# Attention probabilities copied block by block by DMA into F32R slots before they are turned; the merged sum of the branches kept in DRAM

## The chip, the cores and the metric

The kernel runs on one core of a Trainium2 chip. A core has a matrix engine (PE, which loads a 128x128 block of stationary weights and streams moving columns through it; the loads are listed as PEld), a vector engine (DVE), a scalar engine (ACT), a general engine (POOL), and a queue engine (SP) that issues most of the DMAs. PE writes into eight PSUM banks; everything else lives in SBUF (128 partitions) or in DRAM. Engines run side by side, each in the order of its own instructions, and wait for each other by semaphores.

The metric is the device time of one execution in microseconds (us), the median of the runs. Times quoted from the trace come from one profiled execution.

## The reference, cut to what matters

One decoder layer on 512 positions, width 1024. Three mixers read the same normalised input, their outputs are gated and summed, and a feed-forward part follows. The change touches the attention mixer (branch B) and the gated sum:

```python
h = rms_norm(x, g_pre_mix)
z = h @ w_in                      # u, v, q, kv, nsa_g, xr, rg, mg
y_a = gmlp_mixer(...)             # chunked spatial gating
y_b = nsa_mixer(...)              # attention: 16 heads, 4 key/value groups
y_c = rglru_mixer(...)            # linear recurrence

# inside nsa_mixer, for each group of 4 heads and both of "selected" and "window":
s = jnp.where(mask, einsum(q, k) * scale, NEG_INF)
o = einsum(softmax(s), v)
y_b = g0 * o_cmp + g1 * o_slc + g2 * o_win

gates = sigmoid(mg)
merged = gates[0] * (y_a @ w_br_a) + gates[1] * (y_b @ w_br_b) + gates[2] * (y_c @ w_br_c)
x = x + rms_norm(merged @ w_o, g_post_mix)
x = x + rms_norm(swiglu(rms_norm(x)))
```

With 512 positions, 8 selection blocks and a top 16, every block is selected, so the selected and the window attention are both plain causal attention over the same 512 keys, with different key and value projections.

## The kernel before

Everything is kept with channels on the partitions and the 512 positions along the row. Most matrix products are made from two parts of each operand: `split` (L114) has ACT write the rounded part `hi` as type F32R and DVE the remainder `lo`, and three products (hi by hi, hi by lo, lo by hi) replace one exact product. [...]

The program has three phases with their own SBUF and PSUM pools (`PHASES`, `BANKS`). Phase 1 is attention, with two banks `sc` for scores, three `tr` for transposes, one `o` for outputs and two `mm` for other products. Big buffers that live across phases have tags of their own; tag `m` has two buffers of four rows each, and before the change they hold `merged`, the gated sum of the branches, from branch C (phase 0) through attention to branch B (phase 2).

Attention runs over four groups of heads. For each group there are six units of work (class `Unit`, L884): query tile 0 and 1 with both branches at once, tile 2 and 3 with one branch each. A unit has three steps:

- `scores(j)` (L900), for each of its four heads: PE multiplies queries and keys into a bank `sc` (L910), DVE takes the mask and the maximum (L914), ACT the exponential with its sum (L916), all into the buffer `P` (two buffers). After the fourth head DVE makes the factors (L919, L921), and ACT (L926, two heads) and DVE (L930, the others) scale the probabilities in `P`.
- `turn(br, kt)` (L932): for one block of 128 keys, four transposes on PE (L935, one for each head; a "turn" below is one such transpose) from `P` through the f32 identity `ident` into a bank `tr`, which `split` takes apart into `ph` and `pl`.
- `values(br, kt)` (L940): two products with the values `V` into the bank `o` (L948).

A group has 2 + 4 + 3 + 3 + 4 + 4 = 20 blocks, so there are 80 blocks and 320 turns in all.

`attention` (L972) interleaves these steps with the other matrix products that must be made: the projections of the next group and the gates and products of branch A (`fill`). It counts slots, one for each six products of the fill; `LAG_T` is the least number of slots between a unit's last score and its first turn, `LAG_V` that between a block's turn and its product with `V`. Behind that, the framework's scheduler lays out the final order on each engine; rows of it are shown with the change.

SP issues the weight loads (`raw`, two buffers, L182) in the order of `wload`, and the copies between partitions of the queries `q` (L789) and keys `K` (L802).

Branch A's gate is a row of tag `tg` with one buffer in phase 1: ACT writes it (`gate_part`, L1067), DVE multiplies it with the branch's product (`branch_part`, L1079; L1090) and adds it to `merged` (L1091). Behind attention, branch B does the same and splits the sum into `mh` and `ml`, which the output projection reads.

Of the kernel before, what the change touches and what calls it, by code (L numbers as in the profile page):

```python
# [22 lines left out]
F32 = mybir.dt.float32  # L23
# [6 lines left out]
S = 512  # L30
D = 1024
NK = 8
# [18 lines left out]
def hybrid_block(ctx: ExitStack, tc: tile.TileContext, A, out):  # L51
# [18 lines left out]
    def next_banks(i):  # L70
        if psum[0]:
            psum[0].__exit__(None, None, None)
        psum[0] = tc.tile_pool(name=f"psum{i}", bufs=1, space=PSUM, reuse_waits="tile")
        psum[1:] = psum[0].__enter__(), BANKS[i]
# [18 lines left out]
    def slab(name, dt=F32, tag="slab", shape=(4, S)):  # L93
        pool, bufs = (merge if tag == "m" else big, TAGS[tag]) if tag in TAGS else phase_pool[tag]
        return pool.tile([128, *shape], dt, tag=tag, name=nm(name), bufs=bufs)

    def row(name, dt=F32, tag="row"):
        pool, bufs = phase_pool[tag] if tag in phase_pool else (mid, 6)
        return pool.tile([128, S], dt, tag=tag, name=nm(name), bufs=bufs)

    def bank(tag):
        return psum[1].tile([128, S], F32, tag=tag, name=nm(tag), bufs=psum[2][tag])
# [10 lines left out]
    def f32(ap):  # L113
        return ap.bitcast(F32)  # L114

    def split(src, hi, lo, lo_eng=None):
        res["hi"] = SC.activation(hi, src, AF.Copy)  # L117
        e = lo_eng or V
        if e is GP:
            GP.tensor_sub(lo, src, f32(hi))  # L120
        else:
            res["lo"] = V.tensor_sub(lo, src, f32(hi))  # L122
# [761 lines left out]
    class Unit:  # L884

        po = {}

        def __init__(self, g, a, brs):  # L890
            self.g, self.a, self.brs, self.n = g, a, brs, 128 * (a + 1)
            self.blocks = [(br, kt) for br in brs for kt in range(a + 1)]
            self.last = (1, a)
            self.pt = {}

        def part(self, j, br):
            o = self.brs.index(br) * self.n
# [2 lines left out]
        def scores(self, j):  # L900
            g, a, n, brs = self.g, self.a, self.n, self.brs
            w = len(brs)
            if j == 0:
                self.T = slab("P", tag="P")
                self.st = mid.tile([128, 3, 4, w], F32, tag="ast", name=nm("ast"), bufs=3)
            st, K = self.st, at[g]["k"]
            ps = bank("sc")
            lhs = at[g]["q"][:, j, a * 128:(a + 1) * 128]
            for i in range(2):
                PE.matmul(ps[:, :w * n].rearrange("p (b n) -> p b n", b=w), lhs, K[:, i, brs[0]:brs[-1] + 1, :n],  # L910
                          start=(i == 0), stop=(i == 1))
            for b, br in enumerate(brs):
                t = self.part(j, br)
                V.tensor_tensor_reduce(out=t, in0=ps[:, b * n:b * n + n], in1=mask[0][:, S - n:], scale=-0.125,  # L914
                                       scalar=3.0e38, op0=OP.add, op1=OP.min, accum_out=st[:, 0, j, b:b + 1])
                SC.activation(t, t, AF.Exp, scale=-1.0, bias=st[:, 0, j, b:b + 1],  # L916
                              accum_out=st[:, 1, j, b:b + 1])
            if j == 3:
                V.reciprocal(st[:, 2], st[:, 1])  # L919
                gt = gates[:, a, 12 * g:12 * g + 12].rearrange("p (h b) -> p h b", b=3)  # L920
                V.tensor_mul(st[:, 2], st[:, 2], gt[:, :, 1 + brs[0]:2 + brs[-1]])  # L921

                own = 0 if w == 2 else 2
                for i in range(own):
                    t = self.part(i, brs[0])
                    SC.activation(t, t, AF.Copy, scale=st[:, 2, i, 0:1])  # L926
                for b, br in enumerate(brs):
                    o = b * n
                    t = self.T[:, own:4, o:o + n]
                    V.tensor_tensor(t, t, st[:, 2, own:4, b:b + 1].to_broadcast([128, 4 - own, n]), op=OP.mult)  # L930

        def turn(self, br, kt):  # L932
            pt = bank("tr")
            for j in range(4):
                PE.transpose(pt[:, j * 128:(j + 1) * 128], self.part(j, br)[:, kt * 128:(kt + 1) * 128], ident)  # L935
            ph, pl = row("ph", F32R), row("pl", F32R)
            split(pt, ph, pl)
            self.pt[br, kt] = ph, pl
# [23 lines left out]
                    ready.add(g)  # L962

    mask = [None]

    def mask_in():
        mask[0] = slab("mask", tag="mask", shape=(S,))
        GP.memset(mask[0], 0.0)
        GP.affine_select(mask[0][:, 384:], mask[0][:, 384:], pattern=[[-1, 128]], compare_op=OP.is_ge,
                         fill=-1e30, base=0, channel_multiplier=1)  # L970

    def attention(fills):  # L972


        slot = [0]
        LAG_T, LAG_V, LAG_C, LAG_K = 3, 3, 2, 3

        def steps(g, slots):

# [83 lines left out]


    mg = {}

    def gate_part(b, j):  # L1067
        ps = bank("mm")
# [10 lines left out]
    def branch_part(b, j, y):  # L1079

        ps = bank("mm")
        yield from matrix(ps, y["h"], y["l"])
        if "m" not in mg:
            mg["m"] = Pair("merged", tag="m")
        t = mg.pop((b, j))
        m = mg["m"][j]
        if b == "c":
            V.scalar_tensor_tensor(m, t, 1.0, ps, op0=OP.add, op1=OP.mult)
        else:
            V.scalar_tensor_tensor(t, t, 1.0, ps, op0=OP.add, op1=OP.mult)  # L1090
            V.tensor_add(m, m, t)  # L1091
            if b == "b":
                if j == 0:
                    mg["h"], mg["l"] = Pair("mh", F32R, "mo"), Pair("ml", F32R, "mo")
                split(m, mg["h"][j], mg["l"][j])


    def rows_in():
# [555 lines left out]
    def run(main, side=None, rate=1.0, keep=False):  # L1654


        credit = 0.0
        late = []
        for m in main:
            for w in m:  # L1660
                for x in late:
                    x[0] -= 1
                if late and late[0][0] <= 0:
                    if next(late[0][1], 0) == 0:
                        late.pop(0)
                if w:
                    late.append([w, m])
                    break
                credit += rate
                while side is not None and credit >= 1.0:  # L1670
                    credit -= 1.0
                    if next(side, 0) == 0:
                        side = None
            credit += rate
        for _, m in late:
            for _ in m:
                pass
        if side is not None and not keep:
            for _ in side:
                pass  # L1680
# [18 lines left out]
    def qkv(g):  # L1699
        return [q_tile(g, 0), q_tile(g, 1), k_tile(g)] + ([v_pair(g // 2)] if g % 2 == 0 else [])  # L1700
# [23 lines left out]
    for tag in ("sc", "sc", "o"):  # L1724
        bank(tag)
    mask_in()
    run(qkv(0))
    run([], seq(cmp_probs(0)))
    fill = [("a", x) for x in branch("a", ya)]
# [7 lines left out]
    run([], yb_split())  # L1737
    next_phase(2)
    next_banks(2)
    rows_in()  # L1740
    run(branch("b", yb))
    with tc.issue_after(res["tanh"].ins):
# [102 lines left out]
```

## Time and profile before

| | |
|---|---|
| median of 3 runs | 1113.26 us (1112.27 to 1113.33) |
| the profiled execution | 1114.33 us |
| its span, first to last instruction | 1112.6 us |
| attention stage in that span | about 370 to 637 us |
| branch B behind it | 637 to 725 us |
| granted PE clock over the span | 0.998 |

The page gives the busy time of each engine, the chain of work that ended last, followed back from the last instruction, and groups of equal instructions by line. A group's row reads: line, engine, operation, output<-inputs, shapes, count | busy us, mean ns of one | idle time of the engine ahead of it and who ended it. A row of the timeline reads: start in us, length in us, engine, line, operation, count. Lengths of products on PE overlap: each is longer than the step from one start to the next.

### The profile page before, as it was taken

What the parts mean: (1) busy time and instruction counts of PE and PEld (TensorE: products, weight loads), DVE (VectorE), ACT (ScalarE), POOL (GpSimd) and SP (SyncE); (2) the same over time, 40 slices, a digit from 0 to 9 for tenths busy, and PEclk for the clock granted to TensorE, in tenths of its full rate; (3) what the DMA queues carried; (4) which work ended last, traced back from release to release, by engine and by line L of the source; (5) the groups of instructions that cost most, each with busy time, mean ns of one, the idle gap of its engine ahead of it and who ended that gap; (6) DMA issues with size and microseconds to landing.
All of it is one profiled execution on the core that took longest, in us unless ns stands there. A gap on an engine that the chain in (4) does not pass through costs nothing.

```text
span 1112.6 us, 16276 instructions
## 1 busy us (share of the span) xinstructions
PE 1098.5 (99%) x6130; PEld 951.7 (86%) x6130; DVE 848.6 (76%) x1558; ACT 635.1 (57%) x1139; POOL 8.8 (1%) x23
## 2 busy tenths in 40 slices
PE   9999999999999999999999999999999999999997
PEld 7888778888889888898888788888999999998886
DVE  5977959376784888978888844368998888886777
ACT  6757775232344696866867632345655554554663
POOL 1000000100000000000000000000000000000000
PEclk9999999999999999999999999999999999999999
DMA  8445355578653222213121153353232433346253
GB/s 282 131 124 153 88 140 204 209 245 300 219 179 110 79 65 58 67 39 95 48 77 57 39 209 96 113 152 133 96 114 80 130 95 115 98 160 244 81 204 133
DMA packets 49839, 146.25 MB, mean 131 GB/s; under 512 B 9504, under 2 KB 9792, under 8 KB 48736
## 3 DMA queue, kind: packets, MB, share of 16 engines
q1 hardware_dynamic: 44752, 131.28, 36.4%
q10 hardware_dynamic: 4720, 13.24, 4.0%
q8 instruction: 48, 0.79, 0.3%
q0 software_dynamic: 288, 0.69, 0.2%
q14 instruction: 31, 0.25, 0.1%
HBM read 124.22 MB, written 13.63 MB: 124 GB/s over the span
## 4 chain that ended last, share of the span: by engine, by line
PE 85%; DVE 6%; ACT 5%; DMA 3%; issue 1%; SPq 0%; ACTq 0%; DVEq 0%
PE mm L221 37%; PE mm L1345 17%; PE mm L1536 6%; PE mm L549 3%; PE mm L1130 3%; PE sc L910 3%; PE o L948 3%; PE tr L935 2%; PE tr L1536 2%; PE mm L816 2%; PE mm L234 2%; PE tr L715 1%; PE mm L1441 1%; ACT hi L117 1%; DMA raw<-in_w_v 1%
## 5 line engine op out<-in xcount | busy, mean ns | idle before, releaser
L117 ACT ACTIVATE hi<-raw 128x1024 fp32r<-128x1024 f32 (+1 forms) x134 | 137.1, 1023 | 164.6 <-PE mm L221 97.8
L122 DVE TENSOR_TENSOR lo<-raw,hi 128x1024 fp32r<-128x1024 f32 (+1 forms) x134 | 157.8, 1178 | 68.8 <-ACT hi L117 64.1
L221 PE MATMUL mm<-hh,hi 128*128 128x512 f32 x504 | 199.5, 396 | 0.2 <-ACT hi L117 0.2
L221 PE MATMUL mm<-hh,lo 128*128 128x512 f32 x504 | 197.6, 392 | 0.5 <-DVE lo L122 0.3
L221 PE MATMUL mm<-hl,hi 128*128 128x512 f32 x504 | 196.7, 390 | 0.0
L221 PEld LDWEIGHTS mm<-hh,lo 128*128 128x128 f32 x504 | 94.6, 188 | 21.1 <-DVE lo L122 1.5
L221 PEld LDWEIGHTS mm<-hh,hi 128*128 128x128 f32 x504 | 94.7, 188 | 18.7 <-ACT hi L117 0.6
L221 PEld LDWEIGHTS mm<-hl,hi 128*128 128x128 f32 x504 | 94.7, 188 | 18.7 <-issue 0.2
L916 ACT ACTIVATE P<-P,ast 128x128 f32<-128x128 f32 (+3 forms) x128 | 71.0, 556 | 14.4 <-DVE ast L914 13.9
L1345 PE MATMUL mm<-S,g 128*128 128x256 f32 x600 | 77.0, 283 | 0.5 <-ACT fx L1354 0.5
L1345 PEld LDWEIGHTS mm<-S,g 128*128 128x128 f32 x600 | 74.2, 192 | 0.9 <-ACT fx L1354 0.8
L914 DVE CUSTOM_DVE_ANT_0 P<-sc,mask 128x128 f32<-128x128 f32 (+3 forms) x128 | 58.2, 484 | 8.6 <-PE sc L910 8.5
L122 DVE TENSOR_TENSOR pl<-tr,ph 128x512 fp32r<-128x512 f32 x80 | 53.6, 686 | 13.5 <-ACT ph L117 11.5
L117 ACT ACTIVATE ph<-tr 128x512 fp32r<-128x512 f32 x80 | 46.2, 593 | 13.1 <-PE tr L935 10.5
L910 PE MATMUL sc<-K,q 128*128 128x512 f32 (+2 forms) x192 | 49.9, 365 | 0.2
L1345 PE MATMUL mm<-A,g 128*128 128x256 f32 x360 | 46.6, 283 | 0.0
L935 PE MATMUL tr<-ident,P 128*128 128x128 f32 x320 | 45.2, 273 | 0.6 <-ACT P L926 0.6
L935 PEld LDWEIGHTS tr<-ident,P 128*128 128x128 f32 x320 | 38.0, 140 | 8.7 <-ACT P L926 1.4
L1345 PEld LDWEIGHTS mm<-A,g 128*128 128x128 f32 x360 | 44.7, 192 | 0.2 <-DVE fy L1373 0.2
L1345 PE MATMUL mm<-S,hi 128*128 128x256 f32 x240 | 44.6, 283 | 0.0
L1345 PE MATMUL mm<-A,hi 128*128 128x256 f32 x240 | 44.2, 283 | 0.0
L910 PEld LDWEIGHTS sc<-K,q 128*128 128x128 f32 x192 | 33.0, 188 | 6.8 <-DVE ast L914 1.3
(390 smaller groups left out, 2451.4 us busy)
## 6 DMA issues: line engine op xcount, KB each, us to landing
raw<-in_w_in SPq DMA_DIRECT2D x64, 512.0 KB, 3.7
raw<-in_w_fi SPq DMA_DIRECT2D x44, 512.0 KB, 3.6
raw<-in_w_br SPq DMA_DIRECT2D x24, 512.0 KB, 3.7
fo<-in_w_fo SPq DMA_DIRECT2D x18, 512.0 KB, 6.2
sums<-fo SPq DMA_DIRECT2D x18, 512.0 KB, 4.0
raw<-sums SPq DMA_DIRECT2D x18, 512.0 KB, 3.9
raw<-in_w_fo SPq DMA_DIRECT2D x13, 512.0 KB, 3.8
w<-in_cw ACTq DMA_DIRECT2D x4, 1024.0 KB, 5.0
```

What stands on the lines that cost most here:

```text
L117: res["hi"] = SC.activation(hi, src, AF.Copy)
L122: res["lo"] = V.tensor_sub(lo, src, f32(hi))
L221: res["mm"] = PE.matmul(ps[:m, n0:n1], w[:, k * 128:k * 128 + m], x[k][:, n0:n1], start=(t == 0), stop=(t == 3 * NK - 1))
L549: res["mm"] = PE.matmul(b[c], x[k][:, c * 128:(c + 1) * 128], w[:, kk * 512:kk * 512 + 512], start=(k == 0 and t == 0), stop=(k == NK - 1 ...
L910: PE.matmul(ps[:, :w * n].rearrange("p (b n) -> p b n", b=w), lhs, K[:, i, brs[0]:brs[-1] + 1, :n], start=(i == 0), stop=(i == 1))
L914: V.tensor_tensor_reduce(out=t, in0=ps[:, b * n:b * n + n], in1=mask[0][:, S - n:], scale=-0.125, scalar=3.0e38, op0=OP.add, op1=OP.min, a ...
L916: SC.activation(t, t, AF.Exp, scale=-1.0, bias=st[:, 0, j, b:b + 1], accum_out=st[:, 1, j, b:b + 1])
L935: PE.transpose(pt[:, j * 128:(j + 1) * 128], self.part(j, br)[:, kt * 128:(kt + 1) * 128], ident)
L948: PE.matmul(po, VV[:, kt, g % 2, br].rearrange("p i d -> p (i d)"), x, start=(br == 0 and kt == 0 and t == 0), stop=(br == 1 and kt == a a ...
L1130: res["mm"] = PE.matmul(b[c, f], x[k][:, q], w[:, fs], start=(k == 0 and t == 0), stop=(k == NK - 1 and t == 2))
L1345: res["mm"] = PE.matmul(ps, w[:, ks], x[:, l, k, :], start=(first and k == t == 0), stop=(k == 3 and t == 2), skip_group_check=not first)
L1536: res["mm"] = PE.matmul(ps[c], x[:, q], w, start=(start and t == 0), stop=(t == 2), skip_group_check=True)
```

## The change

Three things are done.

- After a unit's scaling, each of its blocks (four heads by 128 keys, 256 KB) is copied from `P` by a DMA on SP into one of eight slots `Pr`. The slots are typed F32R, the DMA writes them as f32, so the bits stay as they are. `turn` transposes from the slot through `idr`, an F32R copy of the identity, and writes the bank as F32R. A turn waits for the copy of its block; a copy waits for the scaling, and for the turns that read the slot eight blocks before.
- `LAG_T` is 4 instead of 3.
- The eight slots take the two buffers of tag `m`. So `merged` leaves SBUF: branch C's gated products are stored row by row to DRAM (`kept[0]`), branch A's to `kept[1]`, both by DMAs of POOL, and `merged_in` loads all 16 rows again behind attention. The addition of branch A moves from attention to branch B.

```diff
 class Unit:
+    count = 0
     ...
     def scores(self, j):
         ...
+            for br, kt in self.blocks:
+                i = Unit.count % 8
+                Unit.count += 1
+                x = turned["P"][i // 4][:, i % 4, :]
+                self.pr[br, kt] = x
+                o = self.brs.index(br) * self.n + kt * 128
+                SY.dma_start(f32(x).rearrange("p (h n) -> p h n", h=4), self.T[:, :, o:o + 128])
     def turn(self, br, kt):
         pt = bank("tr")
+        x = self.pr.pop((br, kt))
         for j in range(4):
-            PE.transpose(pt[:, j * 128:(j + 1) * 128], self.part(j, br)[:, kt * 128:(kt + 1) * 128], ident)
+            PE.transpose(pt[:, j * 128:(j + 1) * 128].bitcast(F32R), x[:, j * 128:(j + 1) * 128], turned["i"])

+turned = {}
+def turned_in():
+    i = turned["i"] = phase_pool["q"][0].tile([128, 128], F32R, name="idr", bufs=1)
+    SC.activation(i, ident, AF.Copy)
+    turned["P"] = [slab("Pr", F32R, "m") for _ in range(2)]

-LAG_T, LAG_V, LAG_C, LAG_K = 3, 3, 2, 3
+LAG_T, LAG_V, LAG_C, LAG_K = 4, 3, 2, 3

+kept = tc.dram_tile([2, NK, 128, S], F32, name="kept")
+def merged_in():
+    m = mg["m"] = Pair("merged", tag="m")
+    for j in range(NK):
+        GP.dma_start(m[j], kept[0, j])
+        mg["a", j] = row("ya")
+        GP.dma_start(mg["a", j], kept[1, j])

 def branch_part(b, j, y):
     ...
+    if b == "c":
+        m = mg["m"][j]
+        V.scalar_tensor_tensor(m, t, 1.0, ps, op0=OP.add, op1=OP.mult)
+        GP.dma_start(kept[0, j], m)
+        return
+    V.scalar_tensor_tensor(t, t, 1.0, ps, op0=OP.add, op1=OP.mult)
+    if b == "a":
+        GP.dma_start(kept[1, j], t)
+        return
     m = mg["m"][j]
-    if b == "c":
-        V.scalar_tensor_tensor(m, t, 1.0, ps, op0=OP.add, op1=OP.mult)
-    else:
-        V.scalar_tensor_tensor(t, t, 1.0, ps, op0=OP.add, op1=OP.mult)
-        V.tensor_add(m, m, t)
-        if b == "b":
-            ...
-            split(m, mg["h"][j], mg["l"][j])
+    with tc.issue_after(res["lo"].ins):
+        V.tensor_add(m, m, mg["a", j])
+    V.tensor_add(m, m, t)
+    ...
+    split(m, mg["h"][j], mg["l"][j])

 mask_in()
+turned_in()
 ...
 next_banks(2)
+merged_in()
 rows_in()
```

Where instructions stand is shown at one unit on three engines, with rows of the built program: line, operation, output<-inputs, size.

On PE, in group 2, the stretch just ahead of the fifth unit's first turn (of four). `sc`, `mm`, `o` and `tr` are the banks, `hh` and `hl` the two parts of the normalised input, `hi` and `lo` those of a weight. Before:

```order
L910 MATMUL sc_4955<-K_4202,q_3843 128x512 x2
L221 MATMUL mm_4971<-hh_128,hi_4700 128x512
L221 MATMUL mm_4971<-hl_130,hi_4700 128x512
L221 MATMUL mm_4971<-hh_128,lo_4701 128x512
L948 MATMUL o_4894<-ph_4919,V_4420 128x512
L948 MATMUL o_4894<-pl_4920,V_4420 128x512
L935 MATMUL tr_4994<-ident,P_4871 128x128 x4
```

With the change:

```order
L957 MATMUL o_4978<-pl_4998,V_4476 128x512
L957 MATMUL o_4978<-ph_5008,V_4476 128x512
L221 MATMUL mm_5044<-hh_129,hi_4744 128x512
L957 MATMUL o_4978<-pl_5009,V_4476 128x512
L221 MATMUL mm_5044<-hl_131,hi_4744 128x512
L221 MATMUL mm_5044<-hh_129,lo_4745 128x512
L911 MATMUL sc_5029<-K_4237,q_3878 128x512 x2
L221 MATMUL mm_5044<-hh_129,hi_4744 128x512
L944 MATMUL tr_5067<-idr,Pr_2812 128x128 x4
```

The first turn has moved back past the next unit's fourth head and more of the fill: between the unit's last score and its first turn stand 16 products of 512 columns and 12 turns before, 28 and 9 now.

On DVE, at the same unit, from the maximum of its last head (L914, now L915) to the scaling of its probabilities (L930, now L931). `P_4871` is the unit's buffer before, `P_4947` now. Before:

```order
L914 ISA P_4871,ast_4872<-sc_4904,mask_2795 128x512
L914 ISA ast_4872 128x1
L122 TENSOR_TENSOR lo_4975<-raw_4972,hi_4974 128x1024
L919 RECIPROCAL ast_4872<-ast_4872 128x4
L914 ISA P_4943,ast_4944<-sc_4945,mask_2795 128x512
L914 ISA ast_4944 128x1
L921 TENSOR_TENSOR ast_4872<-ast_4872,gates 128x4
L122 TENSOR_TENSOR pl_4920<-tr_4914,ph_4919 128x512
L930 TENSOR_TENSOR P_4871<-P_4871,ast_4872 128x1024
```

With the change:

```order
L915 ISA P_4947,ast_4948<-sc_4964,mask_2804 128x512
L915 ISA ast_4948 128x1
L920 RECIPROCAL ast_4948<-ast_4948 128x4
L915 ISA P_5012,ast_5013<-sc_5014,mask_2804 128x512
L915 ISA ast_5013 128x1
L922 TENSOR_TENSOR ast_4948<-ast_4948,gates 128x4
L122 TENSOR_TENSOR pl_4989<-tr_4983,ph_4988 128x512
L931 TENSOR_TENSOR P_4947<-P_4947,ast_4948 128x1024
```

The split of a weight (`lo`) no longer stands ahead of the scaling.

On SP, the queue of the same stretch with the change (before, it held the rows of `q`, `raw` and `K` alone):

```order
L789 DMA q_4740<-q_4740 64x512
L938 DMA Pr_2811<-P_4856 128x4x128 x3
L789 DMA q_4740<-q_4740 64x512
L182 DMA raw_5262<-in_w_br 128x1024
L938 DMA Pr_2812<-P_4947 128x4x128 x4
L938 DMA Pr_2811<-P_5012 128x4x128 x4
L802 DMA K_5043<-K_5043 64x2x512
L182 DMA raw_5347<-in_w_in 128x1024
L802 DMA K_5043<-K_5043 64x2x512
```

A weight load now stands behind the copies of one or two units, and a copy behind a weight load.

More of the change, by code (lines that the diff above doesn't have):

```diff
@@ L893, in __init__ @@
             self.last = (1, a)
-            self.pt = {}
+            self.pt, self.pr = {}, {}
         def part(self, j, br):
@@ L930, in scores @@
                     V.tensor_tensor(t, t, st[:, 2, own:4, b:b + 1].to_broadcast([128, 4 - own, n]), op=OP.mult)
+                for br, kt in self.blocks:
[3 more added lines that the diff above has]
+                    self.pr[br, kt] = x
+                    o = self.brs.index(br) * n + kt * 128
+                    SY.dma_start(f32(x).rearrange("p (h n) -> p h n", h=4), self.T[:, :, o:o + 128])
         def turn(self, br, kt):
             pt = bank("tr")
+            x = self.pr.pop((br, kt))
             for j in range(4):
-                PE.transpose(pt[:, j * 128:(j + 1) * 128], self.part(j, br)[:, kt * 128:(kt + 1) * 128], ident)
+                PE.transpose(pt[:, j * 128:(j + 1) * 128].bitcast(F32R), x[:, j * 128:(j + 1) * 128], turned["i"])
             ph, pl = row("ph", F32R), row("pl", F32R)
@@ L1085, in branch_part @@
         t = mg.pop((b, j))
-        m = mg["m"][j]
-        if b == "c":
-            V.scalar_tensor_tensor(m, t, 1.0, ps, op0=OP.add, op1=OP.mult)
-        else:
-            V.scalar_tensor_tensor(t, t, 1.0, ps, op0=OP.add, op1=OP.mult)
-            V.tensor_add(m, m, t)
-            if b == "b":
-                if j == 0:
-                    mg["h"], mg["l"] = Pair("mh", F32R, "mo"), Pair("ml", F32R, "mo")
-                split(m, mg["h"][j], mg["l"][j])
+        if b == "c":
[7 more added lines that the diff above has]
+            return
+        m = mg["m"][j]
+        with tc.issue_after(res["lo"].ins):
+            V.tensor_add(m, m, mg["a", j])
+        V.tensor_add(m, m, t)
+        if j == 0:
+            mg["h"], mg["l"] = Pair("mh", F32R, "mo"), Pair("ml", F32R, "mo")
+        split(m, mg["h"][j], mg["l"][j])
     def rows_in():
```

## The prediction

> **What bounds the kernel now.** First the page's busy times and its chain of work that ended last, then one window over the attention stage (370 to 637 us) and who PE waited for inside it.
>
> ```profile
> PE 1098.5 (99%) x6130; PEld 951.7 (86%) x6130; DVE 848.6 (76%) x1558; ACT 635.1 (57%) x1139; POOL 8.8 (1%) x23
> ...
> PE 85%; DVE 6%; ACT 5%; DMA 3%; issue 1%; SPq 0%; ACTq 0%; DVEq 0%
> ...
> 370.00:637.00 267.00, 265.34 (x1416) 221.81 (x1415) 230.73 (x566) 198.27 (x476) 0.00 (x0) 1.00 0.21 61
> ...
> PE tr L935 <- ACT P L926: 0.6, 2, 0.3
> PE o L948 <- ACT ph L117: 0.3, 1, 0.3
> PE o L948 <- DVE yb L960: 0.3, 1, 0.3
> PE o L948 <- DVE pl L122: 0.3, 1, 0.3
> ```
>
> The window row reads: length, then busy PE, weight loads, DVE, ACT, POOL, the granted clock (1.00), DMA share, GB/s. PE is busy in 265.34 of 267 us and waits 1.5 us by name. Since ends of products are modelled, I check this by the pace of PE, start to start:
>
> ```profile
> 473.59 1.25 PE L935 MATMUL tr<-ident,P 128*128 128x128 f32 x10
> 637.14 87.04 PE mm L221 x384
> 795.86 184.22 PE mm L1345 x1534
> L221 PE MATMUL mm<-hh,hi 128*128 128x512 f32 x129 | 51.7, 401 | 0.0
> ...
> L935 PE MATMUL tr<-ident,P 128*128 128x128 f32 x320 | 45.2, 273 | 0.6 <-ACT P L926 0.6
> ...
> L865 PE MATMUL tr<-ident,pc 128*128 128x128 f32 x16 | 2.4, 272 | 0.0
> ```
>
> A product with 512 moving columns takes 87.04/384 = 0.2267 us, one with 256 columns 184.22/1534 = 0.1201. Ten transposes take 1.25 us, of which the last one is 0.273: nine steps of 0.1086. The last three rows are the first, the fourth and the last of the stage's 19 groups by shape; with all of them there are 843 products of 512 columns, 64 of 384, 125 of 256, 336 transposes and 48 products of 64 columns (0.108 each, below), at these prices (0.173 for 384) 191.1 + 11.1 + 15.0 + 36.5 + 5.2 = 259 of the 267 us. So PE really stands still about 8 us there. PE binds; DVE, at 86%, is next; the DMA engines are at 21%. What shortens PE's own work in this stage shows in the time unless a wait takes its place.
>
> **The pace of a turn.** The 320 transposes of probabilities lose their f32 operands. What f32 costs in streaming, and what the weight load costs, stands in the rows by line:
>
> ```profile
> L536 PE MATMUL mm<-gw,ones x2: 591/592/592, 234.7 to 235.1; 128*128 128x512 f32 x2
> ...
> L221 PE MATMUL mm<-hh,hi x504: 387/389/791, 57.5 to 717.9; 128*128 128x512 f32 x168
> L935 PEld LDWEIGHTS tr<-ident,P x320: 137/140/144, 378.8 to 634.5; 128*128 128x128 f32 x160
> L221 PEld LDWEIGHTS mm<-hh,hi x504: 186/188/192, 57.3 to 717.7; 128*128 128x128 f32 x168
> 426.91 1.73 PE tr L838 x16
> L838 PE MATMUL tr<-kcb,q x64: 217/275/275, 360.7 to 564.4; 128*128 128x64 f32 x64
> ```
>
> The page prints both types as f32. L536 is a product of plain f32 tiles, L221 of rounded ones (F32R). At 512 columns they take 592 and 389 ns: 203 ns for 512 columns, so 51 ns for 128. A turn would go from 0.1086 to 0.058 us. A second way, the line through 0.2267 and 0.1201 drawn on to 128 columns, gives 0.1201 - 0.0533 = 0.067. I take 0.062: 320 x 0.0466 = **14.9 us** less (16.2 and 13.4 at the two ends). The bound on the other side is no gain at all, if the weight load sets the pace: L838 streams only 64 columns and still takes 1.73/16 = 0.108 us each, behind loads of the 188 ns kind. The load of a turn is 140, shorter by 48, which would allow 0.060. But that short load is seen with f32 alone.
>
> [...]
>
> **What the copies cost.** Each of the 80 blocks now passes through one DMA from SBUF to SBUF of 256 KB, issued by SP. The trace has no such copy with 512-byte pieces; its nearest rows, with the median from issue to landing at the end, and the time that SP spends on one issue:
>
> ```profile
> K<-K SPq DMA_DIRECT2D x8, 256.0 KB, 3.3
> ...
> wabr<-in_wab SPq DMA_DIRECT2D x8, 128.0 KB, 4.3
> q<-q SPq DMA_DIRECT2D x8, 128.0 KB, 3.8
> ...
> L802 SPq DMA_DIRECT2D K<-K x8: 616/621/636, 352.1 to 558.7; - x8
> ```
>
> I take 3.3 (same size, same kind) and keep 4.3, of 256-byte pieces, as the upper end. Whether it is hidden depends on how much PE work stands between a unit's last score and its first turn. The unit that is shown in the order (group 2, fifth unit) reads in the trace of before:
>
> ```profile
> 540.57 0.40 PE L910 MATMUL sc<-K,q 128*128 128x512 f32 x1
> ...
> 546.20 0.60 PE L935 MATMUL tr<-ident,P 128*128 128x128 f32 x4
> ...
> 541.97 1.22 DVE L122 TENSOR_TENSOR lo<-raw,hi 128x1024 fp32r<-128x1024 f32 x1
> ...
> 545.01 1.22 DVE L930 TENSOR_TENSOR P<-P,ast 128x1024 f32<-128x1024 f32 x1
> ...
> 544.73 1.34 ACT L926 ACTIVATE P<-P,ast 128x512 f32<-128x512 f32 x2
> ```
>
> Scaling ends at 546.23, 5.66 us after the last score began, and the turn begins in that moment: this unit has no slack. Afterwards the order holds 28 products of 512 columns and 9 turns between them, 28 x 0.2267 + 9 x 0.062 + 0.23 for the score itself = 7.1 us (before: 16 products, 12 turns, 5.2). The split of 1.22 us no longer stands ahead of the scaling on DVE, so scaling ends after about 4.5; with 3.3 for the copy that is 7.8. PE stops for 0.7 us (1.7 with 4.3). The same subtraction for all 24 units, each with its own times from the trace and its own place in the two orders, leaves a dozen units short, together 8 us with 3.3 and 20 us with 4.3. Since a stop also lets DVE and ACT catch up, the next unit's scaling comes earlier; I take **6 us**, bounds 0 and 20.
>
> SP is in order: a weight load behind four copies is held by their issues, 4 x 0.62 = 2.5 us, and by the wait for the scaling. Its cover:
>
> ```profile
> 614.95 0.33 SPq L182 DMA_DIRECT2D raw<-in_w_in  x1
> 623.39 1.05 ACT L117 ACTIVATE hi<-raw 128x1024 fp32r<-128x1024 f32 x1
> ...
> raw<-in_w_in SPq DMA_DIRECT2D x64, 512.0 KB, 3.7
> ```
>
> The load issued at 614.95 lands about 618.7 and is split at 623.39: 4.7 us to spare. I cost it at nothing; beyond 4.7 us every microsecond of delay stops PE.
>
> **The end of the stage.** Behind the last product of the fill PE has now 24 turns and 18 products with V where it had 12 and 12. That work was only moved there, but each block needs one ACT and one DVE operation before its products, with three banks to hold it:
>
> ```profile
> L122 DVE TENSOR_TENSOR pl<-tr,ph 128x512 fp32r<-128x512 f32 x80 | 53.6, 686 | 13.5 <-ACT ph L117 11.5 <-PE tr L877 1.6
> ...
> L117 ACT ACTIVATE ph<-tr 128x512 fp32r<-128x512 f32 x80 | 46.2, 593 | 13.1 <-PE tr L935 10.5 <-PE o L948 1.1 <-PE tr L877 0.7
> ...
> 631.84 0.39 PE L221 MATMUL mm<-yah,lo 128*128 128x512 f32 x1
> ...
> 636.98 0.39 PE L221 MATMUL mm<-hh,hi 128*128 128x512 f32 x1
> ```
>
> Before, this end took 636.98 - 631.84 - 0.23 = 4.9 us for 12 x 0.2267 + 12 x 0.1086 = 4.0 us of work; twice the blocks, twice the stops: **1 us** more (0 to 3).
>
> **The merged sum in DRAM.** DVE loses eight additions here and has them in the stage behind, whose window is the third row:
>
> ```profile
> L1091 DVE TENSOR_TENSOR merged<-merged,tg 128x512 f32<-128x512 f32 x16 | 11.0, 688 | 0.3
> gw<-in_wsT POOLq DMA_DIRECT2D x1, 256.0 KB, 2.9
> 637.00:725.00 88.00, 88.00 (x390) 72.88 (x389) 39.37 (x48) 29.07 (x36) 0.00 (x0) 1.00 0.39 132
> ```
>
> 8 x 0.688 = 5.5 us of DVE fall under 88 us of PE with DVE at 39.37: nothing on the path; without that cover, 5.5. Sixteen stores and sixteen loads of 256 KB go through POOL's queue, else idle, at about 2.9 us each. The first sum is wanted two matrices of PE work after 637 (48 x 0.2267 = 10.9 us), the first six loads need no more than the slots, which come free with the last turns: nothing, and some 2 us if the loads start late. One ACT copy of the identity: nothing.
>
> **Sum.** The profiled execution took 1114.33 us (span 1112.6). 1114.33 - 14.9 + 6 + 1 = 1106.4; the median of the three runs, 1113.26, lies 1.07 below the profiled one, so **1105.4 us**. With stops between 0 and 12 and the ends of the first term, this case covers 1098 to 1111. Chance 0.50.
>
> **Rivals.**
> Late copies (slower). The copies land like wabr's, or stand behind a waiting weight load, and PE stops at most units: -13.4 + 20 + 1 = +7.6, 1120.9 us. It decides where the stops pass 13.9 us, 0.58 per unit, by the two counts above a copy of 3.8 us, which is q's row. For it: q and wabr, and the units without slack. Against it: K's row, the moved DVE operations, the DMA engines at 21%. Chance 0.17.
> No faster turn. The weight load sets the pace at 0.1086 as for L838, so the change does not do what the types say. The slower turns give more cover (9 x 0.0466 = 0.4 us per unit), stops 3, end 1: 1117.3 us. Against it the load of 140 ns. Chance 0.18.
> DVE takes over. Its 230.7 - 5.5 = 225 us must fit into some 258 instead of 267, in a fixed order; a further 4 us of stops: 1109.4 us. Against it the relief above. Chance 0.15.
>
> **Chances and range.** A measurement of this kernel tells about 0.2%, 2.2 us, from no change. Faster: 0.47 of the forecast's 0.50, 0.13 of DVE's 0.15, 0.03 of no faster turn: 0.63. Within: 0.03 + 0.02 + 0.06, and 0.02 of late copies: 0.13. Slower: 0.15 and 0.09: 0.24. The range 1099 to 1118 leaves out the lowest end of the forecast (0.05) and most of the late copies (0.12).
>
> **What will show it.** Ten turns in a row near 0.62 + 0.2 us of length, not 1.25, show the first term; 0.108 per turn the second rival. PE's waits will name the DMA into the slots ahead of the turns: 6 us in all is right, 14 turns the sign. The landing of these copies (3.3 or 4.3) settles which. The stage should end 7 to 8 us earlier, and the one behind it keep its 88 us; a wait of DVE for the loaded sums there would be an error of mine, as would a wait of ACT for the single gate buffer, or stops of PE at weight splits, which would mean that SP was held up.

## The result and the profile after

| | us | against before |
|---|---|---|
| before, median of 5 | 1113.23 (1112.27 to 1113.33) | |
| changed, median of 5 | 1119.10 (1118.65 to 1119.99) | ratio 1.0056, 95% interval 1.0045 to 1.0067 |
| predicted | 1105.4 (1099 to 1118) | |
| the profiled execution, changed | 1118.65, span 1116.9 (before: 1114.33, span 1112.6) | |

The change costs 5.9 us where a gain of 7.9 was forecast, and the time lies 1.1 us above the range. Rows of the changed kernel by stretch of time (length, busy PE, weight loads, DVE, ACT, POOL, granted clock, share of the DMA engines, GB/s):

```profile
370.00:637.00 267.00, 260.02 (x1396) 213.10 (x1395) 223.67 (x553) 197.19 (x474) 6.48 (x12) 1.00 0.51 149
...
642.00:730.00 88.00, 88.00 (x390) 72.88 (x389) 44.14 (x56) 29.12 (x36) 4.41 (x9) 1.00 0.50 167
```

In the attention stretch PE stood still for 267 - 260.02 = 7.0 us, against 1.7 before, and the DMA engines went from 21% to 51%. The second row is the stage behind: PE is full for its 88 us, as before. So all of it happens in attention, and the first product with ybh, where the next matrices begin, shows how much, before and after:

```profile
642.42 0.39 PE L221 MATMUL mm<-ybh,hi 128*128 128x512 f32 x1
```

```profile
647.18 0.39 PE L221 MATMUL mm<-ybh,hi 128*128 128x512 f32 x1
```

It comes 4.8 us later. Next the groups of the turns on the page of the changed kernel (busy time, mean ns of one, then idle time ahead of them and what ended it), the landing of the copies, and what ended PE's waits in the stage (total, times, longest):

```profile
L944 PEld LDWEIGHTS tr<-idr,Pr 128*128 128x128 f32 x320 | 33.9, 142 | 14.3 <-DMA Pr<-P 4.9
...
L944 PE MATMUL tr<-idr,Pr 128*128 128x128 f32 x320 | 37.3, 246 | 2.7 <-DMA Pr<-P 2.4
...
Pr<-P SPq DMA_DIRECT2D x80, 256.0 KB, 3.0
```

```profile
PE tr L944 <- DMA Pr<-P: 2.4, 4, 1.1
PE o L957 <- DVE yb L969: 1.5, 1, 1.5
PE sc L911 <- DVE ast L915: 1.5, 2, 1.2
PE mm L221 <- DVE V L829: 0.9, 1, 0.9
```

Before, no kind of wait came to more than 0.6 us in all. Now there are four above that: for a copy, for the addition that empties the one bank of the sum (o, 0.3 us before), for DVE's read of a score bank, and for the bank of V. PE itself waits 2.4 us for copies; the 4.9 in the row above are of the weight loads (PEld), which run ahead of PE (the turns' first load starts at 380.5 us, the first turn at 380.7), and don't add to that. The turns did get shorter (mean 246 ns against 273). Here are twelve in a row at the end of the stage, with the stop behind them:

```profile
631.27 0.39 PE L221 MATMUL mm<-yah,lo 128*128 128x512 f32 x1
631.50 0.40 PE L957 MATMUL o<-ph,V 128*128 128x512 f32 x1
631.73 0.39 PE L957 MATMUL o<-pl,V 128*128 128x512 f32 x1
631.96 1.15 PE L944 MATMUL tr<-idr,Pr 128*128 128x128 f32 x12
634.64 0.47 PE L957 MATMUL o<-ph,V 128*128 128x512 f32 x1 [1.53 <-DVE yb L969]
...
641.75 0.39 PE L221 MATMUL mm<-hh,hi 128*128 128x512 f32 x1
```

1.15 us less the 0.25 of the last one is eleven steps of 0.082 us. The prediction said 0.062, the rival 0.108. And the end of the stage, from the last product of the fill (631.27) to the next matrix (641.75), takes 641.75 - 631.27 - 0.23 = 10.3 us; before it took 4.9. Of these 5.4 us more, some 2.2 are work that was moved there (24 turns and 18 products with V, where there were 12 and 12). The stop takes 1.5, and most of the rest goes with a stretch of halved clock (last section).

So three things are to be told apart: what the type gains, what the later turns (LAG_T 4) cost, and what the copies cost.

### The profile page after: what moved, and what is told of

It is laid out like the page before. It is cut to its first block, busy times and chain, and to the rows that moved or that the text cites. A ratio compares the mean times of both kernels' runs of the same rounds, so it can differ in the third digit from the quotient of the medians.

```text
span 1116.9 us, 16642 instructions
## 1 busy us (share of the span) xinstructions
PE 1096.4 (98%) x6130; PEld 945.5 (85%) x6130; DVE 849.6 (76%) x1558; ACT 635.7 (57%) x1140; POOL 26.2 (2%) x55
## 4 chain that ended last, share of the span: by engine, by line
PE 78%; DVE 8%; DMA 6%; ACT 6%; issue 2%; ACTq 0%; DVEq 0%; SPq 0%
PE mm L221 32%; PE mm L1374 17%; PE mm L1565 5%; PE mm L549 4%; PE mm L1159 3%; PE o L957 3%; PE sc L911 2%; DMA Pr<-P 2%; PE tr L1565 2%; PE mm L234 2%; PE tr L944 2%; DVE lo L122 1%; PE tr L715 1%; PE mm L816 1%; PE mm L1470 1%
## 5 line engine op out<-in xcount | busy, mean ns | idle before, releaser
L915 DVE CUSTOM_DVE_ANT_0 P<-sc,mask 128x128 f32<-128x128 f32 (+3 forms) x128 | 58.1, 484 | 12.8 <-PE sc L911 12.6
L944 PEld LDWEIGHTS tr<-idr,Pr 128*128 128x128 f32 x320 | 33.9, 142 | 14.3 <-DMA Pr<-P 4.9
L944 PE MATMUL tr<-idr,Pr 128*128 128x128 f32 x320 | 37.3, 246 | 2.7 <-DMA Pr<-P 2.4
```

The lines of the kernel that those rows point to most:

```text
L944: PE.transpose(pt[:, j * 128:(j + 1) * 128].bitcast(F32R), x[:, j * 128:(j + 1) * 128], turned["i"])
```

## The experiments

The kernel before ran beside each of them, at 1112.9 to 1113.6 us. Differences below are between medians.

**One edit at a time.** First the lag alone and the DRAM alone, both on the kernel before:

```diff
-        LAG_T, LAG_V, LAG_C, LAG_K = 3, 3, 2, 3
+        LAG_T, LAG_V, LAG_C, LAG_K = 4, 3, 2, 3
```

> The kernel before with LAG_T 4 in place of 3 and nothing else: no slots, no copies, no rounded type, merged sum in SBUF. Theory (the copies make the stops, the later turns only lengthen the end of the stage): the clock stays 1.0 throughout and the time is 1 to 2 us above the kernel before, 1114 to 1115.5 us. Rival (the later turns themselves cost it: a burst of turns and products with V at the end of the stage, where one bank holds the sum): 4 to 6 us above, 1117 to 1119 us, with the stop of 1.8 us and the halved clock of the changed kernel at the stage's end.

Measured 1116.82 us (1.0033, 1.0020 to 1.0046): 3.6 us dearer, between the theory (1 to 2) and the rival (4 to 6). The rival's stop is there, though the clock stays at 1.00 through the stage:

```profile
628.61 1.47 PE L935 MATMUL tr<-ident,P 128*128 128x128 f32 x12
631.80 0.47 PE L948 MATMUL o<-ph,V 128*128 128x512 f32 x1 [1.72 <-DVE yb L960]
```

That is the same place as in the changed kernel: twelve turns in one go, then a product that opens the next sum and waits until DVE has emptied the bank of the last one. No copy has part in it. The order brings it about. It is not the whole 3.6 us: this trace is of the shortest execution (1114.64 us), and the other part of the cost isn't placed.

```diff
+    kept = tc.dram_tile([2, NK, 128, S], F32, name="kept")
...
+        if b == "c":
+            m = mg["m"][j]
+            V.scalar_tensor_tensor(m, t, 1.0, ps, op0=OP.add, op1=OP.mult)
+            GP.dma_start(kept[0, j], m)
+            return
```

> The kernel before with the merged sum and the products of branch A in DRAM as in the change, and nothing else of it. Theory (hidden, as the prediction had it): 1113.2 us within 1 us, and the stage behind attention keeps its 88 us. Rival (stores, loads and the moved additions cost time in attention or behind it): 3 to 6 us above, 1116 to 1119 us.

Measured 1113.70 us (1.0000, 0.9991 to 1.0009). The merged sum in DRAM costs nothing that can be told.

**The type without the copies.** The scaling, which writes all the probabilities anyway, writes them into the rounded slab itself:

```diff
-        LAG_T, LAG_V, LAG_C, LAG_K = 4, 3, 2, 3
+        LAG_T, LAG_V, LAG_C, LAG_K = 3, 3, 2, 3
...
-                    V.tensor_tensor(t, t, st[:, 2, own:4, b:b + 1].to_broadcast([128, 4 - own, n]), op=OP.mult)
-                for br, kt in self.blocks:
-                    i = Unit.count % 8
...
-                    SY.dma_start(f32(x).rearrange("p (h n) -> p h n", h=4), self.T[:, :, o:o + 128])
+                    V.tensor_tensor(R[:, own:4, o:o + n], t, st[:, 2, own:4, b:b + 1].to_broadcast([128, 4 - own, n]), op=OP.mult)
```

> The changed kernel without copies: the scaling writes the probabilities straight into a slab of the rounded type in the place of the slots (so their low parts are lost, and pl is zero), LAG_T is 3 again, the merged sum stays in DRAM. Theory (the type gains some 6.5 us, the copies and the later turns lose more): 1106 to 1108 us, turns at 0.086 to 0.09. The prediction's pace of 0.062 would give 1113.2 - 14.9 = 1098.3 us. Rival (the faster turns are given back anyway, since DVE and ACT set the pace): 1111 to 1113 us.

Measured 1107.49 us (0.9947, 0.9935 to 0.9959), 6.2 below the DRAM kernel. From that one it differs by the type and by one thing that comes with it: `P` is free again after the scaling, not only after the turns. No wait of DVE or ACT in the trace of before names the turns as what holds `P`. The price is, by the types in the program, that the probabilities lose their low parts, which the copies keep; no run shows the values. Eight turns and the two products behind them, before and here:

```profile
540.81 1.03 PE L935 MATMUL tr<-ident,P 128*128 128x128 f32 x8
541.60 0.48 PE L948 MATMUL o<-ph,V 128*128 128x512 f32 x1
541.92 0.39 PE L948 MATMUL o<-pl,V 128*128 128x512 f32 x1
```

```profile
615.10 0.80 PE L940 MATMUL tr<-idr,Pr 128*128 128x128 f32 x8
615.74 0.46 PE L221 MATMUL mm<-hh,hi 128*128 128x512 f32 x1
616.05 0.39 PE L221 MATMUL mm<-hl,hi 128*128 128x512 f32 x1
```

Inside the row a step went from 0.1086 to (0.80 - 0.25) / 7 = 0.079 us, which would be 9.5 us for 320 turns. But the first product behind the row now begins 0.09 us after the last turn and not 0.03. From the first turn to the second product, less the 0.227 of one product, a turn costs (541.92 - 540.81 - 0.227) / 8 = 0.110 us before and (616.05 - 615.10 - 0.227) / 8 = 0.090 here. 0.020 x 320 = 6.4 us, and 6.2 were measured. So without copies the gain of the type and its size are shown: two fifths of the 14.9 us predicted. A step inside a row overstates it.

The same with the lag of the change, and then with one step more:

```diff
-        LAG_T, LAG_V, LAG_C, LAG_K = 3, 3, 2, 3
+        LAG_T, LAG_V, LAG_C, LAG_K = 4, 3, 2, 3
```

> The kernel without copies (the scaling writes the rounded type itself) with LAG_T 4 in place of 3. What lies between this and the changed kernel is then the copies alone. Theory (the later turns cost what they cost in plain f32, 3.6 us, at the end of the stage): 1107.5 + 3.6 = 1111 us, and the copies alone take 8 us. Rival (with the shorter turns the later order costs more, PE arrives sooner at the same single bank for the sum): 1114 us or more, copies 5 us or less.

Measured 1109.99 us (0.9970, 0.9958 to 0.9982): the lag costs 2.5 us here, 1.1 less than in f32. In this trace the end of the stage takes 8.7 us for 6.2 us of work, with LAG_T 3 4.9 for 3.8, so the end itself pays some 1.4 of the 2.5. With the copies back, which is the changed kernel, the time is 1119.1: **the copies cost 9.1 us.**

```diff
-        LAG_T, LAG_V, LAG_C, LAG_K = 4, 3, 2, 3
+        LAG_T, LAG_V, LAG_C, LAG_K = 5, 3, 2, 3
```

> The kernel without copies with LAG_T 5. Against the changed kernel with LAG_T 5 (1119.1 us) it tells what the copies cost there. Theory of the latency (one more step covers part of it, and each step costs 2.5 us at the end of the stage): 1112.5 us, so copies 6.6 us against 9.1 with LAG_T 4. Rival (the fifth step costs no more than the fourth, and the copies cost the same 9 us at each lag): 1110 us.

Measured 1112.01 us (0.9988, 0.9977 to 0.9999): another 2.0 us for another step, as the theory had it.

**The copies with plain f32.** Slots, identity and turns in f32, all else as changed:

```diff
-        turned["P"] = [slab("Pr", F32R, "m") for _ in range(2)]
+        turned["P"] = [slab("Pr", F32, "m") for _ in range(2)]
...
```

> The changed kernel with slots, copied identity and turns in plain f32: the copies, the lag and the DRAM stay, only the rounded type goes. Theory (a rounded turn saves 0.02 us each, 0.088 against 0.109): 320 x 0.021 = 6.7 us above the changed kernel's 1119.1, less 1 to 2 us of stops that the slower turns cover: 1123 to 1126 us. Rival (the type changes nothing and the whole difference of the two traces' turns is in their records): 1119 us as the changed kernel, within 1 us.

Measured 1119.31 us (1.0054, 1.0040 to 1.0067). My theory missed by 4 us. Its turns are the slow ones:

```profile
L944 PE MATMUL tr<-idr,Pr 128*128 128x128 f32 x320 | 47.4, 275 | 0.9 <-DMA Pr<-P 0.6
```

275 ns, as before the change, and yet the time is that of the changed kernel. Without copies the type gains 6.2 us, with them nothing (0.2): what a turn saves, PE then loses elsewhere; its waits for copies by name are 0.6 us here and 2.4 in the changed kernel. Against the kernel with the lag alone, the copies cost 2.5 us in f32, and 9.1 with rounded turns.

**Latency, queue or traffic?** The kernel without copies (LAG_T 4) gets the 80 copies back, to a buffer in DRAM that nobody reads:

```diff
+                    x = turned["D"][i // 4][:, i % 4, :]
+                    o = self.brs.index(br) * n + kt * 128
+                    SY.dma_start(f32(x).rearrange("p (h n) -> p h n", h=4), f32(R[:, :, o:o + 128]))
...
+        turned["D"] = [tc.dram_tile([128, 4, S], F32R, name=nm("D")) for _ in range(2)]
```

> The kernel without copies and with LAG_T 4 (1110 us), to which the 80 copies are added again on SP at the same places, but into a DRAM buffer that nobody reads: the turns don't wait for them. It has the queue's waits for the scaling, the issues and the traffic, and not the latency. Theory of the latency (PE waits for the landing, the rest is covered): 1110 to 1112 us. Theory of the queue or the traffic (weight loads and the copies of q and K held up in SP's order, DMA engines shared): 1115 to 1119 us.

Measured 1109.96 us (0.9964, 0.9952 to 0.9976), the time without any copies (1109.99). SP's own waits for the scaling are all there; the longest kind in the changed kernel, and then in this one:

```profile
SPq L938 <- DVE P L931: 98.4, 24, 7.5
```

```profile
SPq L941 <- DVE Pr L934: 98.0, 28, 7.7
```

98 us of waiting at the head of an in-order queue, and the DMA engines as busy as in the changed kernel (the row is below), cost the other work nothing. What they do to the copies themselves this run can't show, since nobody waits for these copies. The trace of the changed kernel can. In all 24 units SP begins the first copy within 0.2 us of the end of the scaling, so no weight load holds it up. One unit, from its scaling on DVE to the turns of a later block:

```profile
482.43 1.21 DVE L931 TENSOR_TENSOR P<-P,ast 128x1024 f32<-128x1024 f32 x1
...
483.70 2.87 SPq L938 DMA_DIRECT2D Pr<-P  x4
...
489.53 0.51 PE L944 MATMUL tr<-idr,Pr 128*128 128x128 f32 x4 [1.14 <-DMA Pr<-P]
```

From issue to landing it is 3.0 us by the median, but up to 6.0; whether the traffic makes the long ones isn't shown. In 9 of the 24 units the first turn begins within 0.3 us of the landing of its copy. So the 9 us come with the turns' dependence on the copies. A row of this kernel, of the one without copies, and of the changed one, each to the end of its stage:

```profile
370.00:632.00 262.00, 259.19 (x1408) 215.30 (x1406) 223.90 (x551) 197.99 (x474) 7.03 (x14) 0.99 0.53 154
```

```profile
370.00:632.00 262.00, 259.29 (x1417) 215.87 (x1415) 224.69 (x556) 198.88 (x477) 7.03 (x14) 1.00 0.24 74
```

```profile
370.00:641.00 271.00, 263.81 (x1415) 215.82 (x1414) 225.97 (x556) 198.88 (x477) 7.45 (x14) 0.99 0.51 149
```

Idle 2.8, 2.7 and 7.2 us, at DMA shares of 0.53, 0.24 and 0.51. So 4.5 of the 9.1 us show as PE standing still. The others don't; the scheduler also gives turns that wait for a DMA another place in the order (below), and what that costs by itself was not measured.

**Other queues.** The copies on POOL's queue:

```diff
-                    SY.dma_start(f32(x).rearrange("p (h n) -> p h n", h=4), self.T[:, :, o:o + 128])
+                    GP.dma_start(f32(x).rearrange("p (h n) -> p h n", h=4), self.T[:, :, o:o + 128])
```

> The changed kernel with its 80 copies issued on POOL's queue in place of SP's, and nothing else. Theory of the queue (on SP the copies and the weight loads hold each other up, since the queue is in order): PE's stops before turns shrink by half and those for late weights go, 2 to 4 us below the changed kernel, 1115 to 1117 us. Theory of the landing (a copy needs 3 us from its issue wherever it is issued): 1119 us within 1.5.

Measured 1137.14 us (1.0222, 1.0208 to 1.0237), outside both theories. The page shows two differences: an issue of such a copy takes 750 ns on POOL, 600 on SP, and a copy lands 3.6 us after it begins, against 3.0. PE's waits for copies, the last row, go from 2.4 to 14.3 us.

```profile
L938 POOL DMA_DIRECT2D Pr<-P x80 | 59.5, 750 | 152.1 <-DVE pl L122 36.7 <-DVE P L931 22.1 <-ACT P L927 19.2
...
Pr<-P POOLq DMA_DIRECT2D x80, 256.0 KB, 3.6
...
PE tr L944 <- DMA Pr<-P: 14.3, 21, 2.2
```

By these the fourth copy of a unit is there 3 x 0.15 + 0.6 = 1.1 us later, and 24 units lose 18 us, 0.75 each. Unintended, this doses the latency, and most of the dose seems to reach the time; that nothing else of POOL's queue has part in it is not shown.

The weight loads of the stage on POOL's queue, the copies on SP's; the stores of branch A's products go to SP as well:

```diff
-                res["ld"] = (SC if i == n == 0 else SY).dma_start(raw[:, p], ap[:, p])
+                res["ld"] = (SC if i == n == 0 else GP if "pool" in res else SY).dma_start(raw[:, p], ap[:, p])
...
-            GP.dma_start(kept[1, j], t)
+            SY.dma_start(kept[1, j], t)
...
```

> The changed kernel with the weight loads of the attention stage issued on POOL's queue, so that the copies have SP nearly alone (the stores of branch A's products go to SP, so that no wait stands ahead of the weights on POOL). Theory of the queue: the loads no longer stand behind waits for the scaling nor the copies behind waits for a free raw buffer, 3 to 6 us below the changed kernel, 1113 to 1116 us. Theory of the latency: 1118 to 1120 us, as the changed kernel.

Measured 1131.61 us (1.0161, 1.0146 to 1.0175), again outside both. The weight loads land later from POOL (4.3 us against 3.8), and PE's waits for copies grew to 8.8 us. It doesn't separate the theories, and why it is so dear stays open.

**More or less lag, with copies,** on the changed kernel.

```diff
-        LAG_T, LAG_V, LAG_C, LAG_K = 4, 3, 2, 3
+        LAG_T, LAG_V, LAG_C, LAG_K = 5, 3, 2, 3
```

> The changed kernel with LAG_T 5, one step of some 3 us more between the scores and the turns. Theory (copies that are too late cost some 7 us, the end of the stage some 3 per step of lag): PE's waits for the slots go from 7.3 us to under 2, the end grows by 2 to 3: 1115 to 1117 us. Rival (the waits are only moved, to the bank of the sum and to the two P slabs): 1119 us or more.

Measured 1119.08 us (1.0045, 1.0031 to 1.0060; executions from 1112.3 to 1120.9). That is the rival's time: PE's waits for copies do not go (2.8 us by name, in two stops).

```diff
-        LAG_T, LAG_V, LAG_C, LAG_K = 4, 3, 2, 3
+        LAG_T, LAG_V, LAG_C, LAG_K = 3, 3, 2, 3
```

> The changed kernel with LAG_T 3, as before the change: copies and rounded type without the extra step. Theory of the latency (a step of some 3 us of cover is gone for 24 units, of which a dozen were short already; 0.5 us each at least): copies cost 15 to 24 us there, 1107.5 + 15 to 24 = 1122 to 1132 us. Rival (the copies cost 9 us by something that the lag doesn't touch): 1107.5 + 9 = 1116.5 us.

Measured 1115.72 us (1.0023, 1.0014 to 1.0032). That is the rival's time. The theory, that a step of lag is 3 us of cover, fails between 3 and 4: the copies cost 8.2, 9.1 and 7.1 us with LAG_T 3, 4 and 5. The 7.1 is a step in its direction, but rests on the medians that spread most.

| median, us | no copies | copies |
|---|---|---|
| f32, LAG_T 3 | 1113.2 | |
| f32, LAG_T 4 | 1116.8 | 1119.3 |
| rounded, LAG_T 3 | 1107.5 | 1115.7 |
| rounded, LAG_T 4 | 1110.0 | 1119.1 (the change) |
| rounded, LAG_T 5 | 1112.0 | 1119.1 |

A part of the reason is in the order of PE. Last score products of the first unit of group 1 and its first turns, without copies and LAG_T 3:

```profile
436.92 0.40 PE L911 MATMUL sc<-K,q 128*128 128x256 f32 x2
...
442.18 0.80 PE L940 MATMUL tr<-idr,Pr 128*128 128x128 f32 x8
```

with copies, also LAG_T 3:

```profile
438.90 0.40 PE L911 MATMUL sc<-K,q 128*128 128x256 f32 x2
...
446.71 0.46 PE L944 MATMUL tr<-idr,Pr 128*128 128x128 f32 x4
```

7.8 us of it against 5.3, with 21 matrix products between in place of 14: the scheduler of the framework, which orders each engine's instructions when the kernel is built, has put work ahead of turns that wait for a DMA. That cover is taken from elsewhere in the stage, and LAG_T asks for it a second time. That this is why more lag doesn't help is argued, not shown.

**The end of the stage, and fewer copies.**

```diff
-                    elif TQ and sdone.get(TQ[0][0], 1e9) + LAG_T <= t and len(TQ) + 3 > len(VQ):
+                    elif TQ and sdone.get(TQ[0][0], 1e9) + LAG_T - (g == G - 1) <= t and len(TQ) + 3 > len(VQ):
```

> The changed kernel with LAG_T 4 for the first three groups and 3 for the last one. Theory (3 us of the loss arise in the burst behind the last filler product): the end of the stage is as long as before the change, with no stop of 1.8 us there, 2 to 3 us below the changed kernel, 1116 to 1117 us. Rival (without the extra step the copies of the last group's six units come too late, 1 us each, and eat it): 1119 to 1123 us.

Measured 1118.41 us (1.0043, 1.0027 to 1.0060): the same as the changed kernel. In the trace, which is of the longest execution (1121.97 us), the wait for the sum's bank is gone (0.3 us in place of 1.5), but PE waits longer elsewhere (3.6 us for copies, 2.3 for score banks). Inconclusive for the end by itself.

```diff
+                SY.dma_start(f32(R[:, :, :w * n]), self.T[:, :, :w * n])
...
```

> The changed kernel with one copy per unit in place of one per block: 24 DMAs of 512 to 1024 KB in place of 80 of 256 KB, into two slabs of the rounded type. Theory of the queue: SP issues 24 and not 80, 2 to 4 us below the changed kernel, 1115 to 1117 us. Theory of the latency: the first block of a unit now waits for the whole unit, by an estimate from 3.0 us for 256 KB and 3.7 for a load of 512 KB some 4 to 5.5 us against 3.0, the last one no longer for four issues: 1119 to 1123 us.

Measured 1115.91 us (1.0025, 1.0014 to 1.0036), as the theory of the queue had it, though the rows above leave the queue little to gain. Of four separate copies the last is issued after three issues of 0.60 us, so it lands about 1.8 + 3.0 = 4.8 us after the first issue; the single one of 1 MB lands after 4.9:

```profile
Pr<-P SPq DMA_DIRECT2D x12, 1024.0 KB, 4.9
```

No earlier, then, and the first block later. Why it is 3 us faster stays open.

Then this with LAG_T 3:

```diff
-        LAG_T, LAG_V, LAG_C, LAG_K = 4, 3, 2, 3
+        LAG_T, LAG_V, LAG_C, LAG_K = 3, 3, 2, 3
```

> One copy per unit and LAG_T 3: the two edits that each took some 3 us off the changed kernel (1119.1 to 1115.9 and to 1115.7), together. If they are independent (issue and landing of the last block of a unit; burst at the end of the stage), 1119.1 - 3.2 - 3.4 = 1112.5 us, which is the kernel before. If both only give the same chain a few us, 1115 to 1116 us.

Measured 1116.57 us (1.0034, 1.0020 to 1.0047): not additive. One copy per unit, LAG_T 3, or both: each lands near 1116, above the kernel before. No version with the copies came down to it.

**The changed kernel once more,** without an edit.

> The changed kernel once more, unchanged, for a second trace: 1119 us. If the halved clock at the end of the stage belongs to every execution, the trace has it again, some 3.4 us long, behind a stop of 1.8 us before the first product with V; if it is chance, the trace lacks it and the time stays within 2 us.

Measured 1118.66 us (1.0054, 1.0037 to 1.0072). The clock stays at 1.00 through attention in this trace, while its span is 1116.1 us, within 0.8 of the first. PE's waits for copies are those of the first trace. The view of the line of the turns adds the idle time of the weight loads; in the first trace and in this one (us, times):

```profile
PE tr L944 <- DMA Pr<-P: 2.4, 5, 1.0
```

```profile
  DMA Pr<-P: 7.3, 18
```

```profile
  DMA Pr<-P: 9.1, 20
```

So the halved clock of the first trace, which the last section shows, isn't what makes the change slower. PE stands still 8.4 us here, to the end of the stage, against 7.2 there: these sums vary by 1 to 2 us from trace to trace.

**What it points to.** The kernel without copies and LAG_T 3 is 5.7 us faster than before and 11.6 faster than the change. Since by the types pl is zero there, one more run leaves out its products with V and the subtractions of DVE that make it:

```diff
-            for t, x in enumerate((ph, pl)):
+            for t, x in enumerate((ph,)):
...
```

> The kernel without copies (LAG_T 3, the scaling rounds) without the low parts pl, which are zero there: 80 products with V of 0.227 us and 80 subtractions of DVE go. If PE is the bound of the stage once no copy stands between, the whole 18.2 us go: 1107.5 - 18.2 = 1089 us. If the chain of scores, exponentials and scaling sets the pace, as it may in the changed kernel, at most half: 1098 us or more.

Measured 1092.03 us (0.9808, 0.9795 to 0.9821): 15.5 of the 18.2 us of PE work reach the time. Without copies PE is the bound of this stage, and ACT doesn't take over; of DVE it says less, since DVE lost work here too.

## Why the prediction was wrong

Going up from the kernel before, one edit at a time, the medians are 1113.2, + 0.5 (DRAM, within the noise), - 6.2 (type), + 2.5 (lag), + 9.1 (copies) = 1119.1. The prediction had nothing, -14.9, +1, and +6. How much falls to which edit depends on the order. By way of f32 (lag 3.6, then copies 2.5, then the type) the same runs give the type 0.2 us and the copies 2.5.

**The pace of a turn: the step that failed most, 8.7 of the 13.7 us.** The sum took a turn from 0.1086 to 0.062 us, by what f32 costs in streaming. The direction is right without copies; the size is not. Steps of 0.079 to 0.082 us came out, and with the product behind a row a turn costs 0.090 after 0.110: 0.020 saved in place of 0.0466. The argument priced the streaming alone, and took the bound by the weight load from the 140 ns of its record. Both limits were too simple: the pair of a load and a turn runs neither at 0.062 nor at the 0.108 of the second rival. And a step inside a row isn't the price of a turn. What sets the steps of 0.079 to 0.082 us is not shown.

**The copies: the wait is there, the price too small, 3.1 us.** The landing was taken at 3.3 us and is 3.0, and PE does stop ahead of turns. But "6 us in all is right" was said of these stops, and they are 2.4 us by name in both traces, while the copies as a whole cost 9.1. That 6 lies within 3 us of 9.1 is in part luck. With a gain of 6.2 in place of 14.9 and the 2.5 of the lag, 9.1 was enough to turn the sign. The prediction counted a unit's own stop only, and even took 2 us off it, "since a stop also lets DVE and ACT catch up". The traces show the contrary: PE then waits for DVE at places where it waited 0.2 us or not at all without copies (1.5 us for score banks and 0.9 for V's bank, above). The rest of the 9.1 us isn't placed. The prediction also priced gains and stops as terms that can be summed. They can't: the f32 slots show that the shorter turn is worth 0.2 us while turns wait for copies. The prediction had that coupling, as 0.4 us of cover per unit, but used it in a rival alone.

**SP in order: right.** It was costed at nothing; 98 us of its waits cost nothing where no turn needs the copies, and in the changed kernel no weight load holds up the first copy of a unit.

**The end of the stage: 1 us taken, 2.5 measured for the lag as a whole** (3.6 in f32), some 1.4 of it at the end. More blocks in three banks were priced; the single bank of the sum was not. With twelve turns in one go, DVE's additions for one sum stand in front of the first product of the next, a stop of 1.5 to 1.7 us.

**The merged sum in DRAM: right,** nothing. The stage behind kept its 88 us, and no wait of PE there came from it.

Of the rivals, no faster turn (1117.3) and late copies (1120.9) lie 1.8 us from the time on either side. Late copies is near by luck: it had copies that land after 4.3 us or behind a waiting weight load, and PE stopping at most units, and none of that came. The rival that kept the turns at their pace was half right: the turns gain without copies, and nothing with them. DVE did not become the bound.

## What to carry to other kernels

Price a short matmul from a stream of loads and matmuls, with the product behind it (0.090 us here, 0.079 inside a row), not from its columns alone (0.062). A DMA put into the middle of a dependent chain (scores, scaling, turn) can cost time (9.1 us here) even where its queue and its traffic cost the other work nothing (1109.96 us against 1109.99); test that by issuing the same copies to a place that nobody reads. If only a type has to change and the low bits can go, let the instruction that writes the data anyway write the new type (1107.49 us here, 1115.72 with copies).

## What the runs showed of the hardware

In the first trace of the changed kernel the granted clock fell to half for 3.4 us, just after the stop at the end of the stage:

```profile
632.00:635.40 3.40, 1.87 (x16) 1.64 (x15) 3.25 (x8) 2.30 (x5) 2.34 (x5) 1.00 0.97 255
635.40:638.80 3.40, 3.40 (x14) 2.58 (x12) 2.61 (x5) 1.45 (x3) 0.34 (x1) 0.50 0.77 249
```

It came right behind a stop of 1.5 us, in a stretch where PE still worked 1.87 of 3.40 us. Products with V begin 0.43 us apart at half clock (635.84 and 636.27 us) and 0.23 ahead of the stop (631.50 and 631.73), so by estimate PE loses 1.7 us in these 3.4. The kernel before has a granted clock of 1.00 through attention. Over the whole span it was 0.998 there and 0.997 in the first trace of the changed kernel, 0.993 in the trace of LAG_T 5 with copies and 0.991 in the one with the weight loads on POOL's queue; the page of that last one has 0.8 in the slice from 565 to 594 us, and 0.9 in its other 39. A stop of about the same length in the second trace of the changed kernel (1.5 us) and in the kernel with the lag alone (1.72 us) left the clock at 1.00 through the stage, so the length of the stop alone doesn't decide; what does isn't shown.

A copy within SBUF on SP's queue lands 3.0 us after its issue at 256 KB and 4.9 at 1 MB (medians).
